# One core, one decoder block: the compressed probabilities of sparse attention as one product of 512 columns, and the steps that prepare it

## The chip, the cores and the metric

The program runs on one core of a Trainium2 chip. The core has a matrix engine (TensorE, PE in the profile), a vector engine (VectorE, DVE), a scalar engine (ScalarE, ACT), a general engine (GpSimd, POOL) and an engine that issues the transfers (SyncE, SP). Each engine works through its own list of instructions in order and waits for the others by semaphores. Products are written to PSUM; all other data lies in SBUF, 128 partitions wide. The metric is the time of one execution on the device in microseconds, as the median of several.

## The reference, cut to what matters

The reference is a decoder block for 256 tokens of width 1024: three token mixers side by side (a sparse attention with 16 heads in 4 groups, a gated recurrence, and an attention over 256 memory tokens), a gated merge, and a SwiGLU channel mixer. The change concerns the sparse attention. Each query has three softmaxes: over 15 compressed blocks, over selected keys and over a window. With at most four blocks of 64 keys, all that causality permits are selected.

```
kc = compress_blocks(k, pe_k, w1_k, w2_k)          # 15 compressed keys a group
vc = compress_blocks(v, pe_v, w1_v, w2_v)
s = einsum('bsghd,bngd->bghsn', q, kc) * NSA_SCALE
p = masked_softmax(s, end[None, :] <= t[:, None])
o_cmp = einsum('bghsn,bngd->bsghd', p, vc)
...
y_nsa = gb[..., 0:1] * o_cmp + gb[..., 1:2] * o_slc + gb[..., 2:3] * o_win
```

## The kernel before, in words

Precision comes from pairs. A value in f32 is split into a high part, which ScalarE rounds by a copy to the type of the matrix engine (fp32r), and a low part, which VectorE gets by a subtraction. A product of two pairs is high by high, high by low and low by high. The helper is `split(hi, lo, src)`. All weights come as 161 transfers of 128 x 1024 elements (`raw`) and are split into `whi` and `wlo`.

The sparse attention runs in eight halves: `nsa_half(g, tb, ...)` for 4 groups `g` and 2 blocks `tb` of 128 queries. A half makes scores (`sc`) for the 4 heads of its group, takes the exponentials (`pc` for the 16 compressed columns, `pp` for the others), scales them by their sums and gates, transposes `pp` block by block (`ptn`), splits the result (`pTh`, `pTl`) and adds the products with the values (`vs`) into one PSUM tile, `pvn`, of 4 heads x 128 queries. In it the lower 64 rows belong to the values' high parts and the upper 64 to their low parts.

The compressed probabilities `pc` lie as 4 heads x 32 columns, of which 16 are used. One transpose (`ptc`) turns them into 128 rows: row 32h + n is head h, block n. ScalarE and VectorE split that into `ch` and `cl`. GpSimd then widens each of the two to 4 heads x 128 queries by a mask of ones and zeros (`bm`, column h is one in rows 32h to 32h + 31), so that head h keeps only its own rows. That gives the two `ce`, and four products of 256 columns (two head pairs, high and low) with `vcs`, the compressed values repeated every 32 rows, add them to `pvn`. ScalarE and VectorE then take `pvn` into `yT` by way of `ylo`.

Between the halves the lists are filled with other work: projections of the other mixers and gates (`pd`, 256 columns a product from `hh`, the normalised input), pieces of the recurrence (`pw`, `pq`, `pn`) and so on.

No order is written out by hand. The program records its operations, and a planner (`Plan`) sorts them for all engines at once by estimated costs, buffers and due times. The table `EARLY` moves single operations, by their number in the recorded list, some nanoseconds ahead or back in urgency. Since nearly all instructions are issued at one line, the profile shows them at L618 (L619 after the change); they are told apart by the names of their tiles. A name with a number, such as `whi_253`, is one use of such a tile.

Of the kernel before, what the change touches and what calls it, by code (L numbers as in the profile page):

```python
# [11 lines left out]
F32 = mybir.dt.float32  # L12
F32R = mybir.dt.float32r
BF16 = mybir.dt.bfloat16
AF = mybir.ActivationFunctionType
ALU = mybir.AluOpType
AX = mybir.AxisListType

P = 128
# [3 lines left out]
NH, NG, HPG, DH = 16, 4, 4, 64  # L23
# [144 lines left out]
class Plan:  # L168
# [363 lines left out]
    MATMUL, SLACK, PASSES = (-3.0, 0.0), (60.0, 130.0), 3  # L532

    EARLY = """
# [11 lines left out]
    """  # L546

    def choose(self):
# [73 lines left out]
def block_kernel(ctx, tc, order, xN, xT, memN, head, cst, vec, row, wg, w1, w2, W, out):  # L622
    plan = Plan(tc)
    PE, ACT, DVE, POOL, SP = (plan.engines[e] for e in ("PE", "ACT", "DVE", "POOL", "SP"))
# [6 lines left out]
    one = pool("one", 1)  # L631
    big = pool("big", 1)
    wpool = pool("wpool", 1)
    work = pool("work", 2)
# [8 lines left out]
    ident = cs[:, K_ID:K_ID + P]  # L643
# [14 lines left out]
    def ps_t(shape, name="pt"):  # L658
        return psum.tile(shape, F32, tag="t", bufs=2, name=name)
# [5 lines left out]
    def split(hi, lo, src):  # L665
        op = ACT.activation(hi, src, AF.Copy)
        DVE.tensor_sub(lo, src, hi.bitcast(F32))
        return op
# [141 lines left out]
    w2t = work.tile([P, 256], F32, tag="ce0", bufs=1, name="w2t")  # L810
# [86 lines left out]
    MC, MT = [msk[:, 384 + 16 * i:400 + 16 * i] for i in range(2)], mtb  # L897


    hid = work.tile([P, 2, NG, 32], F32, tag="ce1", bufs=1, name="hid")  # L900
    POOL.memset(hid, 0.0)
    sts = []
    for j in range(2):
# [103 lines left out]
    vcs = one.tile([P, NG, P], F32R, name="vcs")  # L1007

    pk = ps_t([P, NG, 16], "pk")
    PE.matmul(pk, w2t[:, 0:P], hid[:, 0, :, 0:16], start=True, stop=True)  # L1010
    split(kh[:, :, 256:272], kl[:, :, 256:272], pk)
    pvc = ps_t([P, NG, 64], "pvc")
    hrep = work.tile([P, NG, 4, 32], F32, tag="sq", bufs=3, name="hrep")
    ACT.activation(hrep, hid[:, 1, :, :].unsqueeze(2).to_broadcast([P, NG, 4, 32]), AF.Copy)
    for g in range(NG):
        PE.matmul(pvc[:, g, :], hrep[:, g, :, :], w2t[:, P:192], start=True, stop=True)
    split(vcs[:, :, 0:64], vcs[:, :, 64:128], pvc)
# [194 lines left out]
    ynh = bigt("Y", 2, [P, 8, S], F32R, "ynh")  # L1212
    ynl = bigt("Y", 2, [P, 8, S], F32R, "ynl")
    exps = []
    pcs = [one.tile([P, HPG, 32], F32, name=f"pc{i}") for i in range(2)]
    for t in pcs:
        POOL.memset(t, 0.0)
    bm = cs[:, K_BM:K_BM + 4]
    rvalid = cs[:, K_RV:K_RV + 1]

    def nsa_half(g, tb, qs, yT):
        t = slice(tb * P, (tb + 1) * P)
        pc = pcs[tb]
        pv = ps_v([P, HPG, P], "pvn")
        nkb = tb + 1
        for pr in range(2):
            mx = work.tile([P, 2, 3], F32, tag="mx", bufs=3, name="mx")
            sm = work.tile([P, 2, 3], F32, tag="sm", bufs=3, name="sm")
            pp = work.tile([P, 1024], F32, tag="p", bufs=2, name="pp")
            pv4 = pp[:, 0:512 * nkb].rearrange("p (h b n) -> p h b n", h=2, b=2)  # L1230
            for j in range(2):
                q = qs[:, 2 * pr + j, t]
                if tb == 0:
                    s = ps_s([P, 512], "sc")
                    PE.matmul(s[:, 0:272], q, kh[:, g, P:400], start=True, stop=False)
                    PE.matmul(s[:, 0:272], q, kl[:, g, P:400], start=False, stop=True)
                    sc = ((s[:, P:144], MC[0]), (s[:, 0:P], msk[:, P:256]), (s[:, 144:272], msk[:, P:256]))
                else:
                    s, s2 = ps_s([P, 512], "sc"), ps_s([P, 512], "sc")
                    for x, c, n in ((s, 0, 272), (s2, 272, 256)):  # L1240
                        PE.matmul(x[:, 0:n], q, kh[:, g, c:c + n], start=True, stop=False)
                        PE.matmul(x[:, 0:n], q, kl[:, g, c:c + n], start=False, stop=True)
                    sc = ((s[:, 256:272], MC[1]), (s[:, 0:256], msk[:, P:384]), (s2[:, 0:256], msk[:, 0:256]))

                for b, (x, y) in enumerate(sc):
                    DVE.tensor_tensor_reduce(out=x, in0=x, in1=y, scale=-1.0, scalar=3.0e38, op0=ALU.add, op1=ALU.min,
                                             accum_out=mx[:, j, b:b + 1])
                for b in range(3):
                    out = pc[:, 2 * pr + j, 0:16] if b == 0 else pv4[:, j, b - 1]
                    exps.append(ACT.activation(out, sc[b][0], AF.Exp, scale=-1.0, bias=mx[:, j, b:b + 1],  # L1250
                                               accum_out=sm[:, j, b:b + 1]))
            h0 = HPG * g + 2 * pr
            DVE.tensor_mul(sm, sm, og[:, tb, 3 * h0:3 * h0 + 6].rearrange("p (h b) -> p h b", h=2))
            DVE.reciprocal(sm, sm)
            if tb == 0:
                DVE.tensor_scalar(sm[:, :, 0], sm[:, :, 0], rvalid, None, op0=ALU.mult)
            for j in range(2):
                for b in range(3):
                    o = pc[:, 2 * pr + j, 0:16] if b == 0 else pv4[:, j, b - 1]
                    DVE.tensor_scalar(o, o, sm[:, j, b:b + 1], None, op0=ALU.mult)  # L1260
            for kb in range(nkb):
                pt = ps_t([P, 2, 2, P], "ptn")
                for b in range(2):
                    for j in range(2):
                        n = kb if b or not tb else 1 - kb
                        PE.transpose(pt[:, b, j, :], pv4[:, j, b, n * P:(n + 1) * P], ident)
                th = work.tile([P, 512], F32R, tag="pT0", bufs=2, name="pTh")
                tl = work.tile([P, 512], F32R, tag="pT1", bufs=2, name="pTl")
                split(th, tl, pt.rearrange("p a b c -> p (a b c)"))
                for b in range(2):  # L1270
                    for i, x in enumerate((th, tl)):
                        PE.matmul(pv[:, 2 * pr:2 * pr + 2, :], vs[:, kb, b, g, :], x[:, 256 * b:256 * b + 256],
                                  start=(pr == 0 and kb == 0 and b == 0 and i == 0), stop=False,
                                  skip_group_check=True)
        pt = ps_t([P, P], "ptc")
        PE.transpose(pt, pc.rearrange("p h n -> p (h n)"), ident)
        cl = work.tile([P, P], F32, tag="cl", bufs=1, name="cl")
        ch = work.tile([P, P], F32R, tag="ch", bufs=1, name="ch")
        ACT.activation(ch, pt, AF.Copy)
        DVE.tensor_sub(cl, pt, ch.bitcast(F32))  # L1280
        ce = [work.tile([P, HPG, P], F32R, tag=f"ce{i}", bufs=1, name=f"ce{i}") for i in range(2)]
        for i, x in enumerate((ch.bitcast(F32), cl)):
            POOL.tensor_tensor(ce[i], x.unsqueeze(1).to_broadcast([P, HPG, P]),
                               bm.unsqueeze(2).to_broadcast([P, HPG, P]), op=ALU.mult)
        for pr in range(2):
            for i in range(2):
                PE.matmul(pv[:, 2 * pr:2 * pr + 2, :], vcs[:, g, :], ce[i][:, 2 * pr:2 * pr + 2, :],
                          start=False, stop=(pr == 1 and i == 1), skip_group_check=True)
        ylo = work.tile([64, HPG, P], F32, tag="sq", bufs=3, name="ylo")
        ACT.activation(ylo, pv[64:128], AF.Copy)  # L1290
        for e in range(2):
            DVE.tensor_add(yT[64 * e:64 * e + 64, :, t],
                           pv[0:64].rearrange("p (u e) t -> p u e t", e=2)[:, :, e, :],
                           ylo.rearrange("p (u e) t -> p u e t", e=2)[:, :, e, :])
# [281 lines left out]
```

## Time and profile before

| | |
|---|---|
| time, median of 3 runs | 531.1 us (530.77 to 531.69) |
| the profiled execution's own time | 530.48 us |
| its span, first to last instruction | 528.7 us |
| granted clock of TensorE, mean | 0.999 |
| instructions in the span | 9672 |
| transfers | 97.69 MB, 185 GB/s in the mean |
| ScalarE: weight splits `whi` of 128 x 1024 | 155, 1061 ns each |
| VectorE: weight splits `wlo` of 128 x 1024 | 155, 1231 ns each |
| GpSimd: first and second `ce` of a half | 8 each, 1048 and 1289 ns |

The busy share of an engine counts the time in which at least one of its instructions runs. Products on TensorE overlap, and their ends are modelled, so the sum of their durations is no measure; the distance between starts is. "Idle before" names what ended the time in which an engine had nothing to run. A weight load (PEld) runs beside the product ahead of it.

### The profile page before, as it was taken

The page shows a single profiled execution, that of the slowest core. Times are in us where ns is not written, and L with a number is a line of the kernel's source. Part 1 is how long each engine was busy: PE and PEld are TensorE (multiplying, and loading weights), DVE is VectorE, ACT ScalarE, POOL GpSimd, SP SyncE. Part 2 cuts the span into 40 slices and gives each one's busy share as a digit, 9 for nine tenths or more (in the row PEclk, how much of TensorE's full clock was granted, in tenths as well). Part 3 has the DMA queues.
Part 4 walks back from the last instruction along what each step waited for, and adds up shares of the span by engine and source line. Part 5 has one row for each costly group of instructions (what it writes and reads, how often), then busy time and mean ns, then how long its engine had stood idle before and what let it go on. Part 6 is the DMA issues. An engine that isn't in the chain of part 4 may idle for free.

```text
span 528.7 us, 9672 instructions
## 1 busy us (share of the span) xinstructions
PE 520.1 (98%) x3536; PEld 479.3 (91%) x3536; DVE 421.5 (80%) x915; ACT 348.1 (66%) x689; POOL 26.0 (5%) x37
## 2 busy tenths in 40 slices
PE   8999999999999999999999999999999999999995
PEld 8899998989899999999999998888888888888884
DVE  5799898799998989998987888966776877754543
ACT  6887977566887968876995446655555655554531
POOL 0000000010002021111110000000000000000000
PEclk9999999999999999999999999999999999999999
DMA  8995465536443181346364766635554665555512
GB/s 310 417 359 213 141 239 160 199 121 197 152 153 139 45 287 69 121 145 215 124 211 145 219 219 209 229 120 170 190 199 166 195 205 191 200 199 195 182 62 79
DMA packets 28703, 97.69 MB, mean 185 GB/s; under 512 B 3312, under 2 KB 5232, under 8 KB 28400
## 3 DMA queue, kind: packets, MB, share of 16 engines
q1 hardware_dynamic: 28656, 97.07, 53.8%
q8 instruction: 28, 0.46, 0.4%
q14 instruction: 19, 0.16, 0.1%
HBM read 94.96 MB, written 1.05 MB: 182 GB/s over the span
## 4 chain that ended last, share of the span: by engine, by line
PE 95%; DMA 1%; ACT 1%; POOL 1%; issue 1%; DVE 0%; SPq 0%; DVEq 0%; ACTq 0%
PE pd L618 49%; PE pss L618 33%; PE pvn L618 3%; PE sc L618 2%; PE ptn L618 2%; DMA raw<-in_W 1%; POOL ce L618 1%; PE ph L618 1%; PE ptx L618 1%; PE psm L618 1%; PE pn L618 1%; PE pvm L618 1%; PE pq L618 1%; PE pgf L618 0%; DVE z L618 0%
## 5 line engine op out<-in xcount | busy, mean ns | idle before, releaser
L618 ACT ACTIVATE whi<-raw 128x1024 fp32r<-128x1024 f32 (+1 forms) x159 | 165.8, 1050 | 119.8 <-PE pss L618 50.6
L618 DVE TENSOR_TENSOR wlo<-raw,whi 128x1024 fp32r<-128x1024 f32 (+1 forms) x159 | 192.1, 1218 | 64.9 <-ACT whi L618 64.1
L618 PE MATMUL pd<-hh,whi 128*128 128x256 f32 x800 | 148.6, 281 | 0.0
L618 PEld LDWEIGHTS pd<-hh,whi 128*128 128x128 f32 x800 | 124.2, 189 | 0.3
L618 PE MATMUL pd<-hh,wlo 128*128 128x256 f32 x400 | 112.2, 280 | 0.0
L618 PEld LDWEIGHTS pd<-hh,wlo 128*128 128x128 f32 x400 | 75.3, 188 | 0.0
L618 PE MATMUL pss<-xc,whi 128*128 128x512 f32 x168 | 43.3, 392 | 0.0
L618 PE MATMUL pss<-whi,u 128*128 128x512 f32 x132 | 42.0, 390 | 0.0
L618 PEld LDWEIGHTS pss<-xc,whi 128*128 128x128 f32 x168 | 30.5, 188 | 5.2
L618 PE MATMUL pd<-xc,whi 128*128 128x512 f32 x120 | 31.5, 392 | 0.0
L618 PE MATMUL pd<-whi,hh 128*128 128x512 f32 x96 | 31.4, 397 | 0.0
L618 DVE CUSTOM_DVE_ANT_0 sc<-sc,msk 128x16 f32<-128x16 f32 (+2 forms) x96 | 27.1, 316 | 4.0 <-PE sc L618 3.7
L618 PEld LDWEIGHTS pss<-whi,u 128*128 128x128 f32 x132 | 24.8, 188 | 5.2
L618 ACT ACTIVATE pp<-sc,mx 128x128 f32<-128x128 f32 (+1 forms) x64 | 26.7, 428 | 0.1
L618 PE MATMUL pss<-wlo,u 128*128 128x512 f32 x66 | 25.7, 389 | 0.0
L618 PEld LDWEIGHTS pd<-xc,whi 128*128 128x128 f32 x120 | 22.0, 188 | 3.7
L618 PEld LDWEIGHTS pss<-xc,wlo 128*128 128x128 f32 x168 | 22.4, 188 | 1.8
L618 PE MATMUL pss<-xc,wlo 128*128 128x256 f32 x168 | 22.6, 277 | 0.0
L618 PEld LDWEIGHTS pd<-whi,hh 128*128 128x128 f32 x96 | 17.7, 188 | 3.2
L618 DVE TENSOR_SCALAR pp<-pp,sm 128x256 f32<-128x256 f32 (+1 forms) x72 | 19.8, 316 | 0.1
L618 ACT ACTIVATE pTh<-ptn 128x512 fp32r<-128x512 f32 x24 | 13.5, 599 | 9.5 <-PE ptn L618 9.5
L618 PE MATMUL pd<-wlo,hh 128*128 128x512 f32 x48 | 18.9, 394 | 0.0
(328 smaller groups left out, 1068.6 us busy)
## 6 DMA issues: line engine op xcount, KB each, us to landing
raw<-in_W SPq DMA_DIRECT2D x161, 512.0 KB, 4.1
w<-in_w SPq DMA_DIRECT2D x2, 1024.0 KB, 8.3
xn<-in_xN SPq DMA_DIRECT2D x2, 512.0 KB, 10.3
mn<-in_memN SPq DMA_DIRECT2D x2, 512.0 KB, 8.7
xt<-in_xT SPq DMA_DIRECT2D x2, 512.0 KB, 8.7
kk<-kk SPq DMA_DIRECT2D x8, 128.0 KB, 3.1
x<-in_xN SPq DMA_DIRECT2D x2, 512.0 KB, 4.1
memt<-in_head SPq DMA_DIRECT2D x1, 512.0 KB, 7.7
```

The lines of the kernel that those rows point to most:

```text
L618: op.ins_ = getattr(op.real, op.method)(*map(arg, op.a), **{k: arg(x) for k, x in op.kw.items()})
```

## The change

The compressed probabilities keep 16 columns a head. They are split before the transpose, and high and low parts lie side by side: `pw2` has 4 heads x 2 parts x 16 columns. One transpose, as wide as before, gives rows 32h + 16e + n for head h, part e and block n. ScalarE widens it straight from PSUM in four operations, one for each head: a copy of 128 x 128 scaled by that head's column of `bm`. That makes one `ce` of 4 heads x 128 queries in which high and low parts stand in different rows, and one product of 512 columns with `vcs`, which now repeats the compressed values every 16 rows, adds both. GpSimd takes no part any more.

```
-    hid = work.tile([P, 2, NG, 32], F32, tag="ce1", bufs=1, name="hid")
+    hid = work.tile([P, 2, NG, 16], F32, tag="ce1", bufs=1, name="hid")
...
-    PE.matmul(pk, w2t[:, 0:P], hid[:, 0, :, 0:16], start=True, stop=True)
+    PE.matmul(pk, w2t[:, 0:P], hid[:, 0, :, :], start=True, stop=True)
...
-    hrep = work.tile([P, NG, 4, 32], F32, tag="sq", bufs=3, name="hrep")
-    ACT.activation(hrep, hid[:, 1, :, :].unsqueeze(2).to_broadcast([P, NG, 4, 32]), AF.Copy)
+    hrep = work.tile([P, NG, 8, 16], F32, tag="sq", bufs=3, name="hrep")
+    ACT.activation(hrep, hid[:, 1, :, :].unsqueeze(2).to_broadcast([P, NG, 8, 16]), AF.Copy)
...
-    pcs = [one.tile([P, HPG, 32], F32, name=f"pc{i}") for i in range(2)]
-    for t in pcs:
-        POOL.memset(t, 0.0)
...
-        pc = pcs[tb]
+        pc = work.tile([P, HPG, 16], F32, tag="pc", bufs=2, name="pc")
...
+        pw2 = work.tile([P, HPG, 2, 16], F32R, tag="pw2", bufs=1, name="pw2")
+        split(pw2[:, :, 0, :], pw2[:, :, 1, :], pc)
         pt = ps_t([P, P], "ptc")
-        PE.transpose(pt, pc.rearrange("p h n -> p (h n)"), ident)
-        cl = work.tile([P, P], F32, tag="cl", bufs=1, name="cl")
-        ch = work.tile([P, P], F32R, tag="ch", bufs=1, name="ch")
-        ACT.activation(ch, pt, AF.Copy)
-        DVE.tensor_sub(cl, pt, ch.bitcast(F32))
-        ce = [work.tile([P, HPG, P], F32R, tag=f"ce{i}", bufs=1, name=f"ce{i}") for i in range(2)]
-        for i, x in enumerate((ch.bitcast(F32), cl)):
-            POOL.tensor_tensor(ce[i], x.unsqueeze(1).to_broadcast([P, HPG, P]),
-                               bm.unsqueeze(2).to_broadcast([P, HPG, P]), op=ALU.mult)
-        for pr in range(2):
-            for i in range(2):
-                PE.matmul(pv[:, 2 * pr:2 * pr + 2, :], vcs[:, g, :], ce[i][:, 2 * pr:2 * pr + 2, :],
-                          start=False, stop=(pr == 1 and i == 1), skip_group_check=True)
+        PE.transpose(pt, pw2.rearrange("p h e n -> p (h e n)").bitcast(F32), ident)
+        ce = work.tile([P, HPG, P], F32R, tag="ce0", bufs=1, name="ce")
+        for h in range(HPG):
+            ACT.activation(ce[:, h, :], pt, AF.Copy, scale=bm[:, h:h + 1])
+        PE.matmul(pv, vcs[:, g, :], ce, start=False, stop=True, skip_group_check=True)
```

The table `EARLY` is another one throughout, since the operations have other numbers. Its first entries:

```
-    2:14648000 3:2049450 5:2018550 83:28200 145:2300 149:-2050 150:2350 152:5200 153:6450 160:119500 212:14250
...
+    2:31560350 3:5223550 4:5194000 5:5199950 7:315250 49:483500 81:584700 145:7800 147:3900 150:4100 151:4100
...
```

Three places show what moves. First TensorE, in the first half (group 0, queries 0 to 127), where the compressed probabilities are added. Before, the end of the piece behind the transpose:

```order
L618 MATMUL pvn_1583<-pTl_1637,vs_1291 128x256
L618 MATMUL pd_1650<-whi_1412,hh_416 128x512
L618 MATMUL pvn_1583<-ce0_1640,vcs_1136 128x256
L618 MATMUL pd_1650<-whi_1412,hh_416 128x512
L618 MATMUL pd_1650<-wlo_1433,hh_416 128x512
L618 MATMUL pd_1650<-whi_1412,hh_416 128x512
L618 MATMUL pd_1650<-whi_1444,hh_416 128x512
L618 MATMUL pvn_1583<-ce1_1656,vcs_1136 128x256
L618 MATMUL pvn_1583<-ce0_1640,vcs_1136 128x256
L618 MATMUL pvn_1583<-ce1_1656,vcs_1136 128x256
```

After, all that stands behind the transpose `ptc_1602` up to the product:

```order
L619 MATMUL pd_1557<-whi_1458,hh_402 128x512
L619 MATMUL pd_1557<-whi_1548,hh_402 128x512
L619 MATMUL sc_1608<-kk_1108,qs_1385 128x272 x2
L619 MATMUL pvn_1576<-pTh_1598,vs_1287 128x256
L619 MATMUL sc_1615<-kk_1108,qs_1385 128x256 x2
L619 MATMUL sc_1619<-kk_1108,qs_1385 128x272 x2
L619 MATMUL pd_1557<-wlo_1596,hh_402 128x512
L619 MATMUL pd_1557<-whi_1548,hh_402 128x512 x2
L619 MATMUL pvn_1576<-pTl_1613,vs_1287 128x256
L619 MATMUL pvn_1576<-pTh_1598,vs_1287 128x256
L619 MATMUL pvn_1576<-pTl_1613,vs_1287 128x256
L619 MATMUL pvn_1576<-ce_1606,vcs_1130 128x512
```

Four products in two steps have become one, and what stands between it and the transpose is other work of the same half and of the next.

Then ScalarE in the same half. Before, around the copy `ch`:

```order
L618 ACTIVATE whi_1562<-raw_1419 128x1024
L618 ACTIVATE pTh_1572<-ptn_1548 128x512
L618 ACTIVATE pTh_1624<-ptn_1611 128x512
L618 ACTIVATE ch_1633<-ptc_1617 128x128
L618 ACTIVATE cx_1628<-pd_1454 128x2x256
```

After, from the split of the probabilities to the copy out of `pvn`:

```order
L619 ACTIVATE whi_1569<-raw_1406 128x1024
L619 ACTIVATE pw2_1585<-pc_1472 128x4x16
L619 ACTIVATE pTh_1598<-ptn_1579 128x512
L619 ACTIVATE ce_1606<-ptc_1602,cs_291 128x128 x4
L619 ACTIVATE ylo_1638<-pvn_1576 64x512
```

One operation behind the transpose has become four, and one stands ahead of it.

Last ScalarE at the start of the program, where the first weights (`whi`) and the memory tokens (`mh`) are prepared. Before:

```order
L618 ACTIVATE mh_189<-memt_163 128x256 x2
L618 ACTIVATE whi_234<-raw_204 128x512 x2
L618 ACTIVATE whi_253<-raw_224 128x512 x2
L618 ACTIVATE mh_189<-memt_163 128x256 x4
L618 ACTIVATE whi_291<-raw_261 128x1024
```

After:

```order
L619 ACTIVATE mh_184<-memt_162 128x256 x2
L619 ACTIVATE whi_228<-raw_199 128x512 x2
L619 ACTIVATE mh_184<-memt_162 128x256 x4
L619 ACTIVATE whi_270<-raw_231 128x512 x2
L619 ACTIVATE whi_287<-raw_255 128x1024
```

The third weight block (`whi_253`, now `whi_270`, in two halves) comes behind the last four memory blocks instead of ahead of them; SP issues the two transfers in the new order too.

More of the change, by code (lines that the diff above doesn't have):

```diff
@@ L1248, in nsa_half @@
                 for b in range(3):
-                    out = pc[:, 2 * pr + j, 0:16] if b == 0 else pv4[:, j, b - 1]
+                    out = pc[:, 2 * pr + j, :] if b == 0 else pv4[:, j, b - 1]
                     exps.append(ACT.activation(out, sc[b][0], AF.Exp, scale=-1.0, bias=mx[:, j, b:b + 1],
@@ L1258, in nsa_half @@
                 for b in range(3):
-                    o = pc[:, 2 * pr + j, 0:16] if b == 0 else pv4[:, j, b - 1]
+                    o = pc[:, 2 * pr + j, :] if b == 0 else pv4[:, j, b - 1]
                     DVE.tensor_scalar(o, o, sm[:, j, b:b + 1], None, op0=ALU.mult)
```

21 rows, old and new, of the table EARLY are left out of this document.

## The prediction, made before the change was run

> **What bounds the kernel now.** I read the page's head first, then the busy time by stretches of ten microseconds, then who waited for whom on TensorE.
>
> ```profile
> span 528.7 us, 9672 instructions
> PE 520.1 (98%) x3536; PEld 479.3 (91%) x3536; DVE 421.5 (80%) x915; ACT 348.1 (66%) x689; POOL 26.0 (5%) x37
> ```
>
> ```profile
> 0.00:10.00 10.00, 7.96 (x48) 7.62 (x49) 4.47 (x9) 6.12 (x11) 1.03 (x10) 1.00 0.83 276
> ...
> 160.00:170.00 10.00, 9.84 (x85) 9.40 (x84) 8.40 (x12) 7.87 (x15) 2.19 (x2) 1.00 0.35 118
> ...
> 210.00:220.00 10.00, 9.77 (x85) 9.57 (x84) 9.39 (x39) 9.38 (x34) 3.03 (x2) 1.00 0.37 123
> 220.00:230.00 10.00, 10.00 (x89) 10.00 (x88) 10.00 (x34) 8.38 (x29) 2.05 (x2) 1.00 0.41 134
> ...
> 520.00:530.00 10.00, 2.49 (x11) 1.69 (x10) 2.52 (x6) 1.08 (x3) 0.00 (x0) 0.87 0.30 105
> ```
>
> ```profile
> PE pd L618 <- ACT whi L618: 1.1, 1, 1.1
> PE warm L618 <- POOL mhalf L618: 1.0, 1, 1.0
> PE pvn L618 <- POOL ce L618: 0.4, 2, 0.2
> ```
>
> The second row says 98%. In the table of stretches (after the interval: PE, weight loads, VectorE, ScalarE and GpSimd, busy time and count) TensorE is idle in the first ten microseconds, in the last, and by 0.16 and 0.23 us in two between; all others show 10.00. The three waits above are all that TensorE has. So the span is the time of the instructions on TensorE plus a start and an end. An edit saves what it takes from that stream or from those waits, and costs nothing elsewhere until it makes TensorE wait. Busy TensorE is not a price, though: the ends of its products are modelled and overlap. The price of a product is the distance between starts, and the chain gives it:
>
> ```profile
> 144.34 0.87 PE ptn L618 x8
> ...
> 180.63 10.66 PE pd L618 x94
> ...
> 511.54 5.46 PE pss L618 x24
> ```
>
> The 94 are products of 256 columns: 10.66/94 = 0.113 us each. The 24 have 512 columns: 5.46/24 = 0.2275. A transpose of 128 costs 0.87/8 = 0.109. Other stretches give up to 0.118 for 256 columns.
>
> **Part 1: four products become one.** Eight halves (4 groups by 2 row blocks) each had four products of 256 columns and now have one of 512.
>
> ```profile
> L618 PE MATMUL pvn<-ce,vcs 128*128 128x256 f32 x32 | 6.5, 286 | 0.4 <-POOL ce L618 0.4
> L618 PE MATMUL ptc<-cs,pc 128*128 128x128 f32 x8 | 2.2, 278 | 0.0
> ```
>
> Per half 4 x 0.113 - 0.2275 = 0.226, or with 0.118 0.245; eight times that is 1.8 to 1.95 us. I take **-1.9**. The eight transposes stay, equally wide, so nothing else leaves the stream. The row's 6.5 us must not be used: it holds overlaps and modelled ends.
>
> **Part 2: GpSimd leaves the path.** Two of the eight halves waited for the second GpSimd product:
>
> ```profile
> 161.81 0.28 PE L618 MATMUL pd<-hh,whi 128*128 128x256 f32 x1
> 162.25 0.62 PE L618 MATMUL pvn<-ce,vcs 128*128 128x256 f32 x3 [0.16 <-POOL ce L618]
> 162.71 0.28 PE L618 MATMUL pd<-hh,whi 128*128 128x256 f32 x1
> ...
> 212.60 0.28 PE L618 MATMUL pd<-hh,whi 128*128 128x256 f32 x1
> 213.11 0.61 PE L618 MATMUL pvn<-ce,vcs 128*128 128x256 f32 x3 [0.23 <-POOL ce L618]
> 213.56 0.41 PE L618 MATMUL sc<-kk,qs 128*128 128x272 f32 x2
> ```
>
> ```profile
> 160.17 2.03 POOL L618 TENSOR_TENSOR ce<-cl,cs 128x512 fp32r<-128x512 f32 x1
> ...
> 211.03 2.02 POOL L618 TENSOR_TENSOR ce<-cl,cs 128x512 fp32r<-128x512 f32 x1
> 224.77 1.04 POOL L618 TENSOR_TENSOR ce<-ch,cs 128x512 fp32r<-128x512 f32 x1 [11.71 <-ACT ch L618]
> ```
>
> From 161.81 to 162.25 is 0.44 where 0.113 is due: 0.33 lost; the three products then take 0.46 instead of 0.34, another 0.12. At 212.60 it is 0.40 and 0.11. Together 0.96 us, and in both places the GpSimd product took 2.03 or 2.02 us instead of 1.04. Those products are gone: **-0.95**. What is late next there is ScalarE, part 3. The 0.39 us of idle shown is the lower bound of this term.
>
> **Part 3: four ScalarE operations stand before the product.** The trace has no copy from PSUM with a pointer to a scale, without accumulation and 128 columns wide; nearest is dw, from PSUM with a pointer to a bias:
>
> ```profile
> L618 ACT ACTIVATE dw<-pw,As 128x256 f32<-128x256 f32 x4 | 1.9, 474 | 0.0
> L618 ACT ACTIVATE dw<-pw,As 128x128 f32<-128x128 f32 x4 | 1.5, 368 | 0.0
> ```
>
> ```profile
> 164.82 1.36 ACT L618 ACTIVATE dw<-pw,As 128x256 f32<-128x256 f32 x4
> ```
>
> Two of 256 and two of 128 ran in 1.36 us, not in 1.68: neighbours overlap. Four of 128 are shorter by 2 x (0.474 - 0.368): 1.36 - 0.21 = **1.15 us**. Without overlap they would be 4 x 0.368 = 1.47. How late ScalarE takes up the transposed block is seen from ch, which stood in that place:
>
> ```profile
> 157.94 0.27 PE L618 MATMUL ptc<-cs,pc 128*128 128x128 f32 x1
> ...
> 158.81 0.28 ACT L618 ACTIVATE ch<-ptc 128x128 fp32r<-128x128 f32 x1
> ```
>
> ```profile
> 255.66 0.27 PE L618 MATMUL ptc<-cs,pc 128*128 128x128 f32 x1
> ...
> 256.03 0.28 ACT L618 ACTIVATE ch<-ptc 128x128 fp32r<-128x128 f32 x1 [0.29 <-PE ptc L618]
> ```
>
> These are the latest and the earliest of the eight: 0.87 and 0.37 us after the transpose starts. With 1.15 and 0.05 to hand over (GpSimd's end at 162.20 to the product at 162.25) the product can start 1.57 to 2.07 us after the transpose. The work that hides this is what the new order puts between the two on TensorE; the section on the change shows it for the first half, from behind the transpose to the product. One transpose, five products of 512, six of 256 and four of 272 (0.1205 each by width) make 0.109 + 1.14 + 0.68 + 0.48 = 2.41 us. Counted alike, the eight halves have 2.41, 2.26, 2.05, 2.04, 4.67, 2.38, 2.26 and 2.83. Against 1.57 nothing is lost; against 2.07 0.05 us in all; against 2.39 (late and without overlap) 0.13 + 0.34 + 0.35 + 0.01 + 0.13 = 0.96. I take **+0.2**, near the dw row.
>
> The Trainium skill, ScalarE: Activation LUTs, section What ACT_TABLE_LOAD costs, speaks against four small operations with pointers: it gives 186 ns plus 0.833 ns an element, 93 ns more for a pointer, and an overlap of 93 ns. By it four would take an estimated 4 x 386 - 3 x 93 = 1265 ns, and the term would be +0.28 at the latest start; the dw rows agree in kind and lie 0.1 us lower.
>
> **Part 4: other load.** ScalarE loses ch and gains four ce and one pw of 64 columns:
>
> ```profile
> L618 ACT ACTIVATE ch<-ptc 128x128 fp32r<-128x128 f32 x8 | 2.2, 279 | 1.5 <-PE ptc L618 1.5
> L618 DVE TENSOR_TENSOR cl<-ptc,ch 128x128 f32<-128x128 f32 x8 | 2.3, 285 | 0.3 <-ACT ch L618 0.3
> L618 ACT ACTIVATE kk<-pk 128x64 fp32r<-128x64 f32 x1 | 0.2, 197 | 0.0
> L618 DVE TENSOR_TENSOR kk<-pk,kk 128x64 fp32r<-128x64 f32 x1 | 0.2, 218 | 0.0
> ```
>
> That is 1.15 + 0.2 - 0.28 = 1.07 us more ScalarE work a half, 8.6 in all, between 100 and 280 us. It is hidden as long as weight splits run ahead of TensorE; if not, up to 8.6 would show, beyond even the slower rival below; since TensorE waited for a weight split only once, before 8.99 us, I cost it at 0. VectorE swaps 0.285 for 0.218, which frees 0.5 us. Its busiest stretch above is already at 10.00 of 10, and GpSimd worked beside it for 2.05 us there, so it gains rather than loses. The new split must end before the transpose: pw waits for the last scaling of pc, VectorE's subtraction for pw, the transpose for both. Behind pw on ScalarE waits a pTh, behind the transpose all of TensorE. The narrower hid and pc, the other repetition in hrep and the dropped memsets cost nothing: they stand on GpSimd and ScalarE ahead of work that TensorE reaches much later.
>
> **Part 5: the order moves.** The new table moves instructions on every engine. At the start of ScalarE, shown in the section on the change, the third weight block's halves moved behind the four memory blocks, as their DMAs did on SP. In the trace of before:
>
> ```profile
> 8.31 2.36 ACT L618 ACTIVATE whi<-raw 128x512 fp32r<-128x512 f32 x4 [1.32 <-DMA raw<-in_W]
> 10.80 1.71 ACT L618 ACTIVATE mh<-memt 128x256 fp32r<-128x256 f32 x4
> ```
>
> ```profile
> 11.96 0.64 PE L618 MATMUL pd<-mh,whi 128*128 128x256 f32 x4
> ```
>
> Two halves end at about 9.5, where the third block's data was there; the transfer that now stands in its place should be there too. The four memory blocks then end at 11.2 and the first half of the third block 0.6 later at 11.8: just ahead of its first product at 11.96. The price is 0, at worst some 0.3. The wait of 1.05 us before 8.99 stays, since the same first weight transfer ends it. For the rest of the new order I take **+0.2**; its ends are 0 (as in before, outside the named waits) and 1.05, one more wait like that one.
>
> **Sum.** -1.9 - 0.95 + 0.2 + 0.2 = -2.45 us. The profiled execution took 530.5 us, 528.7 of it span, which gives 528.0; it lies 0.6 under the median of 531.1, which gives **528.6**.
>
> **Rivals.**
> - *The waits go further down.* Parts 3 and 5 cost nothing, and the wait at the start shortens too: -1.9 - 0.95 - 1.05 gives 527.2. The same DMA order up to the first weight block speaks against it. Chance 0.10.
> - *ScalarE comes late in the tight halves.* Its queue is in order, and a weight split lasts 1.06 us. If one slips ahead of ce where ch came at once, the product is ready at 2.63: 0.22 + 0.37 + 0.58 + 0.59 + 0.25 + 0.37 = 2.4 us lost. The sum is then -1.9 - 0.95 + 2.4, about 530.7. For it: ScalarE was busy for 9.38 of 10 us in one stretch above. Against: a late weight split cost TensorE only once, at the start. Chance 0.14.
> - *Slower.* The same split ahead of a ce that was already late makes it 3.13: 0.72 + 0.87 + 1.08 + 1.09 + 0.75 + 0.87 + 0.30 = 5.7 us lost, and 533.9. It decides from 2.88 us on, where the eight losses are 3.9 and the sum passes +1.06; ScalarE would have to start 1.7 us after the transpose, and the latest in before was 0.87. Chance 0.05.
> - *The change doesn't do what it says.* TensorE's stream shrinks, but VectorE, full between 220 and 230, sets the pace and TensorE waits for wlo instead. The 1.9 us are given back, and the time is about 530.3. Against: no such wait stands in the list. Chance 0.09.
>
> The forecast itself has 0.62. A measurement can tell about 0.2%, some 1.06 us, from no change. The range 527.2 to 530.8 takes in the forecast, the first rival, the last and the upper end of the late ScalarE. **Faster** by more than 0.2%, under 530.0: 0.78; **within**: 0.17; **slower**, over 532.2: 0.05.
>
> **What would show it.** Right: 8 products pvn<-ce of 512 columns about 0.2275 us apart from what follows, no wait of TensorE for GpSimd, four ce in about 1.15 us starting 0.4 to 0.9 after the transpose, and TensorE's stretches at 10.00 from 20 to 520 us. Wrong: waits "PE pvn <- ACT ce" of over 0.1 us a half (part 3), a wait of ptc for VectorE's pw (part 4), or new waits for whi or wlo in places that the edit doesn't touch (part 5).

## The result, and the profile after

| | before | changed |
|---|---|---|
| median, 4 runs each | 531.36 us (530.77 to 531.69) | 526.94 us (526.28 to 527.69) |
| ratio, with its 95% interval | | 0.9918 [0.9901, 0.9936] |
| the profiled execution's own time | 530.48 us | 527.69 us |

The kernel became 4.4 us faster, and 2.45 had been forecast; 526.94 lies below the range of 527.2 to 530.8. Two executions among the experiments further down ran far slower than all others, one of e1 (644.68 us) and one of e5 (1338.91 us): they are in the medians of the table there, which would be 526.46 and 528.56 us without them, and not in the ratios. The profiled execution of before was its fastest, that of the changed kernel its slowest, so the two profiles lie only 2.8 us apart.

The page's head after the change:

```profile
span 525.9 us, 9588 instructions
PE 517.4 (98%) x3512; PEld 475.5 (90%) x3512; DVE 417.3 (79%) x915; ACT 353.9 (67%) x720; POOL 6.2 (1%) x19
```

TensorE has 24 products less, and GpSimd's 20 us are gone. The waits of TensorE in this profile (engine, what it waited for, us, times, longest):

```profile
PE pd L619 <- ACT whi L619: 1.2, 1, 1.2
PE warm L619 <- POOL mhalf L619: 1.0, 1, 1.0
```

Only the two at the start are left. The two stretches of ten microseconds in which TensorE had waited for `ce` (the columns are those of before):

```profile
160.00:170.00 10.00, 10.00 (x88) 9.90 (x87) 9.84 (x32) 9.90 (x34) 0.00 (x0) 1.00 0.18 65
...
210.00:220.00 10.00, 10.00 (x88) 9.95 (x87) 9.80 (x34) 9.46 (x26) 0.00 (x0) 1.00 0.31 107
```

Both are full now, although ScalarE is busy for 9.90 and 9.46 of 10. The groups of instructions that the edit made, and one half in the order of time (transpose, the four copies, the product):

```profile
L619 PE MATMUL pvn<-ce,vcs 128*128 128x512 f32 x8 | 3.1, 393 | 0.0
L619 ACT ACTIVATE ce<-ptc,cs 128x128 fp32r<-128x128 f32 x32 | 9.1, 379 | 1.0 <-PE ptc L619 0.9
L619 ACT ACTIVATE pw<-pc 128x64 fp32r<-128x64 f32 x8 | 2.1, 263 | 1.0 <-DVE pc L619 0.9
```

```profile
150.70 0.28 PE L619 MATMUL ptc<-cs,pw 128*128 128x128 f32 x1
```

```profile
151.28 1.15 ACT L619 ACTIVATE ce<-ptc,cs 128x128 fp32r<-128x128 f32 x4
```

```profile
153.05 0.39 PE L619 MATMUL pvn<-ce,vcs 128*128 128x512 f32 x1
```

The four copies start 0.58 us behind the transpose, end 1.15 later at 152.43, and the product is due at 153.05: 0.62 us to spare. That is what the prediction had worked out. It explains 2.85 of the 4.4 us (1.9 of columns, 0.95 of waits). A further part is not in any wait, and not near the edit. It is in the merge of the three mixers, a stage in which both kernels compute the same. The chain of work in that stage (start, duration, operation, count), before:

```profile
293.98 11.31 PE pss L618 x96
305.29 5.65 PE pd L618 x48
```

and after:

```profile
291.18 10.88 PE pss L619 x96
302.06 5.44 PE pd L619 x48
```

The same 144 products of 256 columns take 16.96 us before and 16.32 after: 117.8 ns from start to start against 113.3. TensorE has two paces for such products, and in these two profiles the whole stage has one or the other. In the changed kernel the pace turns at one instruction. TensorE around the last half's product:

```profile
272.96 0.28 PE L619 MATMUL pss<-ymemt,wlo 128*128 128x256 f32 x1
273.08 0.28 PE L619 MATMUL pss<-ymemt,whi 128*128 128x256 f32 x1
273.20 0.39 PE L619 MATMUL pvn<-ce,vcs 128*128 128x512 f32 x1
273.43 0.28 PE L619 MATMUL pss<-ymemt,whi 128*128 128x256 f32 x1
...
273.90 0.28 PE L619 MATMUL pss<-ymemt,wlo 128*128 128x256 f32 x1
```

Ahead of the wide product the starts are 0.12 us apart, and from 273.9 on 0.113, up to 312.8 us: 345 products, 345 x 4.44 ns = 1.5 us.

### The profile page after: what moved, and what is told of

It reads as the page before. It is cut to its first block, busy times and chain, and to the rows that moved or that the text cites. A ratio compares the mean times of both kernels' runs of the same rounds, so it can differ in the third digit from the quotient of the medians.

```text
span 525.9 us, 9588 instructions
## 1 busy us (share of the span) xinstructions
PE 517.4 (98%) x3512; PEld 475.5 (90%) x3512; DVE 417.3 (79%) x915; ACT 353.9 (67%) x720; POOL 6.2 (1%) x19
## 3 DMA queue, kind: packets, MB, share of 16 engines
HBM read 94.96 MB, written 1.05 MB: 183 GB/s over the span
## 4 chain that ended last, share of the span: by engine, by line
PE 93%; DMA 2%; DVE 2%; ACT 1%; issue 1%; SPq 0%; DVEq 0%; ACTq 0%
PE pd L619 50%; PE pss L619 31%; DMA raw<-in_W 2%; PE pvn L619 2%; PE sc L619 2%; PE ptn L619 2%; DVE wlo L619 1%; PE ph L619 1%; PE ptx L619 1%; PE pn L619 1%; PE pvm L619 1%; PE psm L619 1%; ACT whi L619 1%; PE pq L619 1%; DVE xt L619 0%
## 5 line engine op out<-in xcount | busy, mean ns | idle before, releaser
L619 PE MATMUL pd<-hh,whi 128*128 128x256 f32 x800 | 147.1, 281 | 0.0
L619 PE MATMUL sc<-kk,qs 128*128 128x272 f32 (+1 forms) x96 | 18.1, 292 | 0.0
```

The source lines that it names most:

```text
L619: op.ins_ = getattr(op.real, op.method)(*map(arg, op.a), **{k: arg(x) for k, x in op.kw.items()})
```

## The experiments

In short; each ratio is to before, measured on the same chip. e1 to e4, e5 to e8 and e9 to e11 ran on three different chips, so between these groups the ratios compare better than the medians:

| run | what | median us | ratio, 95% interval |
|---|---|---|---|
| e1 | the changed kernel again | 526.51 | 0.9915 [0.9900, 0.9931] |
| e2 | before again | 531.26 | 0.9996 [0.9985, 1.0008] |
| e3 | the edit in the old order | 532.11 | 1.0016 [1.0008, 1.0025] |
| e4 | new order, four products in every half | 530.42 | 0.9985 [0.9977, 0.9994] |
| e5 | new order, four products in the last half only | 528.63 | 0.9951 [0.9937, 0.9964] |
| e6 | changed, last product one place earlier | 528.10 | 0.9944 [0.9931, 0.9958] |
| e7 | e3, last product one place later | 530.96 | 1.0001 [0.9989, 1.0014] |
| e8 | changed, three products moved | 525.66 | 0.9897 [0.9883, 0.9910] |
| e9 | before, one wide product in the last half | 530.25 | 0.9979 [0.9969, 0.9989] |
| e10 | changed, last product one place later | 526.74 | 0.9914 [0.9901, 0.9927] |
| e11 | changed, GpSimd widens again | 528.29 | 0.9943 [0.9931, 0.9955] |

The first four put three theories of the missing 2 us against each other: EDIT (they come with the edited instructions, wherever these stand), ORDER (they come with the new order), DRAW (the paces fall by chance in each execution).

### The two kernels again

> The changed kernel once more, to narrow the ratio and to have a second trace of it. Theory EDIT (the edited instructions bring the whole 4.4 us in any order, by freeing VectorE from GpSimd): ratio 0.990 to 0.993. Theory ORDER (the edited instructions bring the 2.85 us of the sum, -1.9 for columns and -0.95 for the waits, and the new order brings the other 1.6 by letting more products of 256 columns run at 113 ns from start to start instead of 118): the same ratio. Theory DRAW (the change is worth the 2.8 us between the two profiled executions, the medians of four differ by more because of the executions drawn): 0.994 to 0.996. Share of products of 256 columns at 116 ns or more, 0.49 in the first trace: ORDER expects 0.44 to 0.54 again, DRAW expects it to move by 0.1 or more from one execution to the next.

> The kernel before once more, as a control. All theories: ratio 0.998 to 1.002. Share of products of 256 columns at 116 ns or more, 0.61 in the first trace: ORDER expects 0.56 to 0.66 again, DRAW expects it to move by 0.1 or more.

Both came out as at first, and so did the paces. Of all products of 256 columns in the trace (leaving out those over 125 ns from the next start, where something else comes between), those 116 ns or more from the next are 49% in both executions of the changed kernel and 61 and 62% in those of before. DRAW falls: in these executions the pace belongs to the program.

Two waits do differ from one execution to the next. The one for the first weights, 1.2 us in the changed kernel's profile above, is shorter in e1's:

```profile
PE pd L619 <- ACT whi L619: 0.6, 1, 0.6
```

And e2 has one behind the merge, near 340 us, which the profile of before does not have:

```profile
PE pss L618 <- ACT xc L618: 0.4, 1, 0.4
```

TensorE waits there for `xc` in four of the six traces in the order of before (e2, e3, e7, e13: 0.2 to 0.9 us), and in none of those of the new order.

### The edit without the new order

```
-            POOL.tensor_tensor(ce[i], x, bm, op=ALU.mult)      # twice, ch and cl
+            for h in range(HPG): ACT.activation(ce[:, h, :], pt, AF.Copy, scale=bm[:, h:h + 1])
-                PE.matmul(pv[:, 2 * pr:2 * pr + 2, :], vcs[:, g, :], ce[i][...])     # four times
+            PE.matmul(pv, vcs[:, g, :], ce)                    # where the fourth stood
```

The calls are shortened here, and the split of the probabilities ahead of the transpose is not shown. Everything else stands in the places, buffers and addresses of before.

> The edited instructions put into the instruction order of before: the split pair ahead of the transpose, four ScalarE copies in the place of ch, one product of 512 columns in the place of the last of the four, no GpSimd; everything else, the buffers and their addresses too, stands as in before. In one half the transpose and the copies come 1.1 us later, since the pair would not be ready. EDIT: -4.4 us, ratio 0.990 to 0.993. ORDER and DRAW: -1.9 -0.95 = -2.85 us, ratio 0.9946 (0.993 to 0.996); in the trace no wait of TensorE for GpSimd and 24 products fewer.

It gained nothing, 0.75 us over before and 5.6 over the changed kernel, as no theory had expected. One reason is in its list of waits (four waits for ScalarE's exponentials `pp` and copies `cx`, 1.1 us of idle) and in ScalarE's order of time:

```profile
195.57 0.61 ACT L647 ACTIVATE pTh<-ptn 128x512 fp32r<-128x512 f32 x1
196.05 1.16 ACT L1339 ACTIVATE ce<-ptc,cs 128x128 fp32r<-128x128 f32 x4
197.05 0.54 ACT L647 ACTIVATE pp<-sc,mx 128x256 f32<-128x256 f32 x1
```

```profile
197.72 0.52 PE L647 MATMUL sc<-kk,qs 128*128 128x272 f32 x2 [0.28 <-ACT pp L647]
```

The four copies are on time for their own product, but an exponential stands behind them, and TensorE waits for the score buffer that it empties. Against the changed kernel it also lacks the fast pace: the merge stage kept the slow one, as a row of the chain of work shows:

```profile
294.59 11.31 PE pss L647 x96
```

### The new order with narrow products

```
-        PE.matmul(pv, vcs[:, g, :], ce, start=False, stop=True)
+        for i in range(2):
+            for pr in range(2):
+                c = slice(2 * pr, 2 * pr + 2)
+                PE.matmul(pv[:, c, :], vcs[:, g, :], ce[:, c, :], start=False, stop=(i == 1 and pr == 1))
```

> The changed kernel with four products of 256 columns, back to back, in the place of each product of 512, all else in the order of the change; the compressed part is added twice. It prices the columns alone. All theories: 8 x (4 x 0.113 to 0.118 - 0.2275) = +1.8 to +1.95 us against the changed kernel. If columns were worth less than that, the gain lies in the waits or the order.

Order, buffers and ScalarE's work are those of the changed kernel; the time is 3.5 to 3.9 us higher than its two medians, not the 1.9 of the columns. Its merge stage, in the chain of work:

```profile
292.80 11.31 PE pss L646 x96
```

So the new order with narrow products does not have the fast pace, and the edit in the old order does not have it either. That gave a sharper theory, STEP: a pace holds until something of another width comes between, and one wide product of the edit, in its place in the new order, turned it.

### Only the last half

> The changed kernel, order and buffers as they are, with one edit: in the last of the eight halves (its product started at 273.20 us) the product of 512 columns is four of 256 again (the compressed part of that half is added twice, so its values differ). Theory STEP: TensorE has two paces for products of 256 columns, 113.3 and 117.8 ns from start to start, a pace holds until something of another length comes between, and it was the wide product at 273.20 us that took the 345 products of the merge stage (273.7 to 312.8 us) from 117.8 to 113.3. Then the merge stage runs at 117.8 here: 345 x 4.44 ns = 1.5 us, and 4 x 117.8 - 233 ns = 0.24 us for the columns, so 1.8 us more than the changed kernel's 526.5 to 526.9, that is 528.4 us, ratio to before 0.995. Theory ORDER (the pace comes from the whole new order or from where buffers lie, not from this product): only the columns, 0.24 us, ratio 0.992.

528.63, where STEP said 528.4. The profile is from a further run of the kernel, e12.

> The same kernel as the one with the last half in four products, for a profile: theory STEP expects the merge stage at 117.8 ns per product, theory ORDER 113.3 ns.

It took 528.54 us, and the chain of work shows the merge stage at

```profile
291.51 11.31 PE pss L646 x96
```

One product of 512 columns instead of four of 256, in one half of eight, is worth 1.7 to 2.1 us here (against the two medians of the changed kernel), of which 0.24 is its own and 1.5 lies in products that follow.

### Places

Two weight loads in the trace of the changed kernel (mean ns of one at the end), first the one ahead of the product at 273.20, then the one ahead of the product at 234.94:

```profile
L619 PEld LDWEIGHTS pvn<-ce,vcs 128*128 128x128 f32 x1 | 0.2, 188 | 0.0
```

```profile
L619 PEld LDWEIGHTS pvn<-ce,vcs 128*128 128x128 f32 x1 | 0.2, 192 | 0.0
```

The second left the pace slow. At the slow pace loads repeat 188, 188, 192; at the fast one all are 188. So the slow pace has a period of three products, and STEP says that the place in the period decides. That can be tested by a swap of neighbours.

```
 pss<-ymemt,wlo 128x256
-pss<-ymemt,whi 128x256
 pvn<-ce,vcs    128x512
+pss<-ymemt,whi 128x256
```

> The changed kernel with the same instructions; only the last half's wide product (273.20 us) changes places with the product of 256 columns just ahead of it, on TensorE alone. In the traces so far, where a wide product stands between products at the slow pace, weight loads repeat 188, 188, 192 ns, and every wide product whose own load was the 192 (234.94 us in the changed kernel, 279.59 us in the old order) took 236 ns and left the pace slow, while those whose load was a 188 took 231 or 233 ns and left it fast. One place earlier the load is the 192. Theory STEP therefore expects 236 ns for this product, the merge stage at 117.8 ns, 345 x 4.44 ns = 1.5 us more than the changed kernel, 528.2 us, ratio 0.9943. Theory ORDER expects no difference from a swap of two neighbours: 526.5 to 526.9 us, ratio 0.9915, merge stage at 113.3 ns.

> The changed kernel with the last half's wide product (273.20 us) one place later on TensorE, the other way than in the run before. Its weight load is then the second 188 behind the 192. Theory STEP: 230 or 231 ns, as at 153.05 and 206.38 us, and the pace turns fast: no change of time, 526.5 to 526.9 us, ratio 0.9915, merge stage at 113.3 ns. If instead any move of that product costs the merge stage its pace: 528.1 us, ratio 0.9944.

528.10 for one place earlier, 526.74 for one place later; both as STEP had them to 0.1 us. The load ahead of the wide product in the first, and a row of its chain in the merge stage:

```profile
L644 PEld LDWEIGHTS pvn<-ce,vcs 128*128 128x128 f32 x1 | 0.2, 193 | 0.0
```

```profile
290.95 11.31 PE pss L644 x96
```

and the same row of the second's chain:

```profile
290.57 10.88 PE pss L644 x96
```

Identical instructions, one product moved by two places, no wait for it in either: 1.4 us. The same in the old order, where the last product's load was the 192:

```
 pss<-ymlt,whi  128x256 x2
-pvn<-ce,vcs    128x512
 pss<-ymlt,wlo  128x256
+pvn<-ce,vcs    128x512
```

> The edit in the old order (ratio 1.0016, 532.1 us, merge stage at 117.8 ns) with the last half's wide product, which stood at 279.59 us with a load of 192 ns ahead of it and took 236 ns, behind its next neighbour of 256 columns, on TensorE alone. Its own load is then the 188 that follows the 192. Theory STEP expects 233 ns for it and the rest of the merge stage (about 280.2 to 318 us, some 320 products) at 113.3 ns: 320 x 4.44 ns = 1.4 us less, 530.7 us, ratio 0.999. Theory ORDER expects 532.1 us, ratio 1.0016.

The chain of work in the merge stage:

```profile
295.37 10.88 PE pss L672 x96
```

The pace turned. The time went down by 1.15 us between the medians, by 0.8 between the ratios (e3 ran on another chip); the intervals allow the 1.4 expected.

### The pace without the change

```
-                # last half, high part: two products of 256 columns (pr = 0 and 1)
+                PE.matmul(pv, vcs[:, g, :], ce[0])      # one of 512, where the first stood
```

> The kernel before with one edit: in its last half one product of 512 columns (the whole high part) stands where the first of its four products of 256 stood (277.80 us, a weight load of 188 ns behind one of 192), and the third of the four is gone; the columns computed are the same, all else is as before. Theory STEP: the wide product takes 233 ns and turns the pace, so the rest of the merge stage (277.9 to some 317 us, about 335 products) runs at 113.3 ns: 335 x 4.44 ns = 1.5 us less than before, 529.8 us, ratio 0.997. Theory ORDER (the pace of that stage belongs to the new order): no difference to before, 531.2 us, ratio 1.000.

0.9979: 1.2 us less, about what STEP says. But this kernel's profile was taken at a granted clock of 0.948, and there the pace turned fast behind the wide product and fell back 2 us later, between two products of 256 columns. So it was profiled again:

> The kernel before with one wide product in its last half again, for a profile at the full granted clock (the first one was taken at 0.948 and its pace fell back from 113 to 118 ns two us behind the wide product, between two products of 256 columns). Theory STEP: the wide product takes 230 to 233 ns and the merge stage from there to about 317 us runs at 113.3 ns. If the pace falls back here too, the time of 530.25 us has another cause than the merge stage.

The same row of its chain:

```profile
293.15 10.89 PE pss L645 x96
```

At a clock of 0.999 the fast pace held through the stage. The run (e13) took 530.74 us, one execution of before on its chip 531.74. So most of the 1.5 us, 1.2 in e9, could be had in the old kernel with one wide product and nothing else of the change.

### GpSimd again

```
-        for h in range(HPG):
-            ACT.activation(ce[:, h, :], pt, AF.Copy, scale=bm[:, h:h + 1])
+        ACT.activation(ch, pt, AF.Copy)
+        POOL.tensor_tensor(ce, ch.unsqueeze(1).to_broadcast([P, HPG, P]),
+                           bm.unsqueeze(2).to_broadcast([P, HPG, P]), op=ALU.mult)
```

> The changed kernel with its order and its product of 512 columns, but the widening put back on GpSimd: ScalarE copies the transposed block once to SBUF, and one GpSimd product per half makes ce. The chain behind the transpose is then the start of ScalarE's copy (0.3 to 1.1 us behind it), about 0.4 us of copy, and 1.04 us of GpSimd, or 2.03 us where VectorE is busy, against 1.15 us for the four copies; the product follows the transpose after 2.11 us or more. Theory WAITS (the two waits for GpSimd fell away because ScalarE's copies are shorter): TensorE waits for GpSimd's ce again, in one to four halves, 0.4 to 2.5 us in all, ratio 0.9925 to 0.996. If the new order alone took the waits away: no wait for ce, ratio 0.9915.

Ratio 0.9943, 1.4 to 1.8 us over the changed kernel's two medians. Three views of it: its waits for GpSimd, one of the two GpSimd products behind them, and TensorE in the order of time there:

```profile
PE pvn L647 <- POOL ce L1312: 0.8, 2, 0.5
```

```profile
189.24 1.98 POOL L1312 TENSOR_TENSOR ce<-ch,cs 128x512 fp32r<-128x512 f32 x1 [11.93 <-ACT ch L1311]
```

```profile
190.51 0.28 PE L647 MATMUL pd<-hh,whi 128*128 128x256 f32 x1
191.27 0.50 PE L647 MATMUL pvn<-ce,vcs 128*128 128x512 f32 x1 [0.48 <-POOL ce L1312]
191.61 0.28 PE L647 MATMUL pd<-hh,whi 128*128 128x256 f32 x1
```

From 190.51 to 191.27 is 0.76 where 0.113 is due, and 0.34 follow where 0.23 are. Even with one GpSimd product a half and the new order, two halves wait, each time behind a product of 1.9 to 2.0 us instead of 1.05. The waits went because of ScalarE's copies, not because of the order; e3, with the copies in the old order, has no wait for `ce` either.

### A faster version

```
 pd<-wlo,hh     128x512             # at 90.87 and at 122.78 us
-pd<-whi,hh     128x512
 pd<-hh,...     128x256 x6
+pd<-whi,hh     128x512
...
-pvn<-ce,vcs    128x512             # at 234.94 us
 pd<-hh,whi     128x256
+pvn<-ce,vcs    128x512
```

> The changed kernel with three products of 512 columns moved on TensorE, nothing else: the last product of the output projection's groups at 90.87 and at 122.78 us goes behind the six products of 256 columns that follow it, and the wide product at 234.94 us (load of 192 ns, 236 ns, pace stays slow) goes behind its next neighbour. Theory STEP: each then stands behind a load of 188 ns among products at the slow pace and turns it fast; the stretches behind them are 83, 92 and 64 products long, so 239 x 4.44 ns = 1.1 us less than the changed kernel: 525.6 us, ratio 0.9895, if the paces further down come out as they did. They need not: a pace that arrives other than before can turn the later ones, and if the merge stage comes out slow it is 527.1 us. Theory ORDER: 526.5 to 526.9 us, and the three stretches at 117.8 ns.

525.66 us, ratio 0.9897, below both kernels. Its interval overlaps with that of the changed kernel; its four executions (525.30 to 526.28) lie at or below the fastest of the changed kernel's (526.28). The stretches behind the three places, in the chain of the changed kernel:

```profile
87.60 14.13 PE pd L619 x105
...
115.75 18.72 PE pd L619 x128
...
235.33 7.66 PE pd L619 x65
```

and of this one:

```profile
86.59 13.77 PE pd L644 x105
...
114.38 18.33 PE pd L644 x128
...
233.68 7.27 PE pd L644 x64
```

0.36, 0.39 and 0.28 us (of the last, one product went ahead of the stretch): 1.03 of the 1.1 expected. The merge stage kept its fast pace.

## Why the prediction missed

By its own steps, against 4.4 us measured:

- **Part 1, columns, -1.9: right.** In e4 all eight products are narrow again. Its 3.5 to 3.9 us are the 1.9 and the merge stage's 1.5, with 0.1 to 0.5 left over.
- **Part 2, waits for GpSimd, -0.95: right.** They are gone, and e11 brought two back.
- **Part 3, +0.2: right in its working, nothing of it due.** The copies took 1.12 to 1.16 us a half, where 1.15 was derived from `dw`. The estimate of 1265 ns from the Trainium skill, ScalarE: Activation LUTs, section What ACT_TABLE_LOAD costs, lies 0.1 above them. They started 0.31 to 1.09 us behind the transpose, a wider spread than the 0.37 to 0.87 of `ch`, and the earliest product came 2.11 us behind it. None waited.
- **Part 4, 8.6 us more on ScalarE at no cost: right for the new order, not as a rule.** The reason given, that TensorE waited for a weight split only once, looked at one kind of ScalarE's work. In e3 it was the exponentials that came late. Of the 3.6 us that e3 lies above before minus 2.85, the list of waits names 1.1 for `pp` and `cx` and 0.6 for `xc`, which executions of before wait for as well. Idle is a lower bound: added up, the late starts of the `sc` products from 190 to 262 us cost e3 an estimated 2.8 us more than before, by the distances in the two traces.
- **Part 5, +0.2 for the rest of the order, ends 0 and 1.05: this step failed.** The start cost nothing, as said. But for everything else the range had no end below zero: moved instructions were taken to cost a wait or nothing. The pace of 113 or 118 ns stood in the prediction, as a spread within which to price 32 products. That it was two values, each held over hundreds of products, and that the edit and the order could turn it for a stage, was not asked. The chain of before had the rows: 94 products at 0.113 and, further down, 96 at 0.118. The missing term is -1.5 us in the merge stage, shown by e5 (with e12's trace), e6 and e10.
- **Sum.** -1.9 - 0.95 - 1.5 = -4.35, against -4.4. This closes better than it should, and partly by luck. In other stretches the paces moved too, some up, some down. Over all products of 256 columns the starts lie 7.1 us above 113 ns each in before and 5.9 after, so about 0.3 us went the other way outside the merge stage. And the wait for `xc` is in no term. From the first `pgf` product to the end of the span, with the same products of TensorE ahead of it in both, before takes 487.8 us and the changed kernel 484.6 and 484.3 in its two traces: 3.3 to 3.6 us less. e2, an execution of before with that wait, takes 489.5. So part of the 4.4 us lies there. The prediction had been read from an execution without the wait. No run tests whether the new order removes it, and its share stays open.
- **The rivals.** "The waits go further down" had a time near the measured one, 527.2, by a wait at the start that shortens. It is 1.2 us in the first profile and 0.6 in e1's, but varies as much in the old order: 1.1 in before, 0.4 in e3. Nothing shows that the order shortens it. ScalarE came late in no half. VectorE set no pace.

That the product of 512 columns turned the pace in the merge stage is shown, by a swap of neighbours. What in TensorE makes the two paces is not.

## What to carry to other kernels

Where an engine is full, read from the chain what one instruction costs from start to start, stage by stage: if like instructions have two values, ask what sets which, because an edit far away may change it. Before a change is credited with its gain, undo it in one place only, and swap two neighbours: here a third of the gain was the place of a single product, and one wide product gave the old kernel 1.2 us of it. Read more than one trace of a kernel: the wait for `xc` stood in four of six, and not in the one that the prediction was made from. Work that is moved to a busy engine must be followed to whatever is queued behind it there, not only to the one wait that the list shows.

## What the runs showed of the hardware

- Products of 256 columns in fp32r start 113.3 or 117.8 ns apart (10.88/96 and 11.31/96), with a weight load for each. The Trainium skill, TensorE: Matmul & The Clock Gate, section Back-to-back issue gap, gives N/2.4 + 2.5 ns as the gap of an isolated product, by which 256 columns would take an estimated 109. The runs have two, both above it.
- A single product of 512 columns between products of 256 turns the pace, by a rule without exception in the 43 cases of these traces with six products of 256 ahead and behind (some fifteen places in the kernels, half of them seen in several traces; e5's trace is not used): at the fast pace it turns it slow (16 of 16); at the slow pace it turns it fast if its own weight load is one of 188 ns (20 of 20), and leaves it if it is the 192 (7 of 7). From its start to the next are then 225 to 227, 230 to 234, and 236 ns. Not among the 43 are the two wide products of e11 that waited: one of them, with a load of 187 ns, left the pace slow.
- Transposes of 128 columns turn the pace as well: at 274.51 us in before one stands between products 113 and 118 ns apart, and the pace then stayed slow into the merge stage. When they do was not worked out.
- The pace can fall back without any such instruction: in one execution (e9's profile), at a granted clock of 0.948, 2 us behind the wide product. Whether the clock is the cause was not tested.
